# Filling TensorE's early waits with products of the identity, in a fused MLA, Hyena and MoE layer

## Chip, cores and metric

The kernel runs on one core of one Trainium2 chip. The metric is the device time of one execution in microseconds (us); lower is better. One execution was profiled; its times are counted from the first instruction of its span.

## What is computed

One layer of a diffusion backbone over 512 latent tokens and 256 context tokens of width 1024, all in f32. The part that the change touches is the very beginning:

```python
mod  = (silu(c) @ w_mod + b_mod).reshape(B, 6, D)
modc = (silu(c_ctx) @ w_mod + b_mod).reshape(6, D)
h  = modulate(rmsnorm(x, norm_mix), mod[:, 0], mod[:, 1])
hc = modulate(rmsnorm(ctx, norm_mix), modc[0], modc[1])
proj = h @ w_in + b_in
...
attention, Hyena convolution, merge, router, 64 experts, final norm
```

The change adds products whose result nobody reads; what is computed stays the same.

## The kernel before

The program is one long unrolled kernel. Tiles are allotted from pools, and the framework derives every wait from the tiles that an instruction reads and writes. A tile that lies in PSUM takes one bank. The order of instructions on each engine is laid out when the program is built, by a planner that simulates times. While `pinned[0]` is true, though, TensorE's products and transposes that go through the helpers `mm` (line 92) and `flip` (line 95) keep the order in which the code names them, and so do the loads that go through `fetch` (line 191). ScalarE's and VectorE's instructions are not held in this way.

The stage in question is the first 60 us. The code names it in one list (lines 374 to 425). For each q from 0 to 7:

- `mod_load(q)` fetches two tiles `wm` of 512 KB with 256 columns of `w_mod`. Six such tiles exist, so three q's can be under way.
- `mod_rows(q)` (line 207) multiplies silu of both conditioning vectors by those columns. The product `pm` is split into four groups of 32 output partitions (`mod_parts`, eight calls of `mm`; an f32 product is two passes on TensorE, each with a weight load, so 16 passes are recorded). ScalarE copies `pm` into a slice of `tit` (line 213). Two further products `ptm` with `cols32` (line 216, four passes) sum the four groups and turn the row into columns. VectorE adds the bias into `sh` (line 217).
- the pool `pm` has one bank, so the next q's products wait until the copy has read it.

The order of the q's on TensorE is 0, 4, 1, 5, 2, 6, 3, 7: shift and scale of the same 256 columns come one after the other. After each pair, `scales(k)` makes the factors `A`, and `streams(k, "l")` and `streams(k, "c")` transpose two column blocks of the normed tokens against the identity (`pxl`, eight passes; `pxc`, four), apply shift and scale on ScalarE (line 336), and split them into a high and a low part (lines 105 and 106). `both_mm(j)` (tiles `p`) multiplies the split tokens by two blocks of `w_in`, in twelve products of 512 or 256 columns in the type fp32r. Products `ps` belong to a small sine layer. `normed("l")` works on ScalarE and VectorE and precedes `mod_rows(0)`; TensorE has nothing to do before that. `ident` is a 128x128 f32 identity that GpSimd builds at the start.

Products with the identity as the moving operand occur elsewhere too: `srkv` and `srq` (line 477) multiply a 128x128 f32 tile by `ident`. In `mix` (line 815) one PSUM tile is cut in two halves of 256 columns: `po` is copied out by ScalarE at line 828, and then products with `ident` write the other half.

Of the kernel before, what the change touches and what calls it, by code (L numbers as in the profile page):

```python
# [51 lines left out]
def kernel(ctx: ExitStack, tc: tile.TileContext, x, ctxt, wmod, bmod, win, wuq, wuk, wuv, wba, wbh,  # L52
# [24 lines left out]
    def bank(name, n=512, tag="b1"):  # L77
        p, bufs = pspool[tag]
        return p.tile([128, 512], F32, name=name, tag=tag, bufs=bufs)[:, :n]
# [7 lines left out]
    def pin(i):  # L87
        if pinned[0]:
            tc.keep_in_program_order(i)

    def mm(o, lhsT, rhs, start=True, stop=True):
        pin(pe.matmul(o, lhsT, rhs, start=start, stop=stop))  # L92
# [26 lines left out]
    ident = const.tile([128, 128], F32, name="ident")  # L119
# [6 lines left out]
    def v(col, n=1, p=128):  # L126
        return vec[:p, col:col + n]

    def rsqrt(pool, ms, name):

        shp = list(ms.shape)
        a = pool.tile(shp, F32, name=name + "_a", tag="rq_a", bufs=2)
        s = pool.tile(shp, F32, name=name + "_s", tag="rq_s", bufs=2)
        r = pool.tile(shp, F32, name=name + "_r", tag="rq_r", bufs=4)
        dve.tensor_scalar(a, ms, EPS, None, ALU.add)
        act.activation(s, a, AF.Sqrt)
        dve.reciprocal(r, s)
        dve.tensor_tensor(s, r, r, ALU.mult)
        dve.tensor_tensor(s, s, a, ALU.mult)
        dve.tensor_scalar(s, s, -0.5, 1.5, ALU.mult, ALU.add)  # L140
        dve.tensor_tensor(r, r, s, ALU.mult)
        return r
# [39 lines left out]
    def mod_parts(pm, w):  # L182


        for j in range(8):
            g = 32 * (j % 4)
            mm(pm[g:g + 32], sc32[:, j], w(j), j < 4, j >= 4)

    def fetch(dst, src):

        tc.keep_in_program_order(sp.dma_start(dst, src))

    def mod_load(q):
        wmt[q] = [mp.tile([128, 4, 256], F32, name=f"wm{q}{h}", tag="wm", bufs=6) for h in range(2)]
        for h in range(2):
            fetch(wmt[q][h], wmod[q, :, 4 * h:4 * h + 4])
# [8 lines left out]

    pinned[0] = True

    def mod_rows(q):
        pm = bank(f"pm{q}", 256, "pm")
        mod_parts(pm, lambda j: wmt[q][j // 4][:, j % 4, :])  # L210

        row = tit[:, q % 4].rearrange("p r c -> p (r c)")
        act.copy(row, pm)
        pt = bank(f"ptm{q}", 4, "ms")
        for i in range(2):
            mm(pt[:, 2 * i:2 * i + 2], row[:, i * 128:(i + 1) * 128], cols32[:, 0:2])
        dve.tensor_tensor(sh[:, 2 * q:2 * q + 2, :], pt.rearrange("p (i c) -> p i c", c=2),
                          v(V_BM + 2 * q, 2).unsqueeze(2).to_broadcast([128, 2, 2]), ALU.add)
# [95 lines left out]
    def normed(nm):  # L314
        na = 2 * len(xs[nm])
        ms = mp.tile([128, na], F32, name=f"ms{nm}")
        for a in range(na):

            sq = (hT if nm == "l" else hTc)[1][:, 0:D // (128 * na)].rearrange("p j n -> p (j n)")
            act.activation(sq, xs[nm][a // 2][:, a % 2], AF.Square, scale=1.0 / 32.0, accum_out=ms[:, a:a + 1])  # L320
        rs = rsqrt(mp, ms, f"rs{nm}")
        for a in range(na):
            xi = xs[nm][a // 2][:, a % 2]
            dve.tensor_scalar(xi, xi, rs[:, a:a + 1], None, ALU.mult)
# [57 lines left out]
    for d, src in ((embt, emb), (w1t, fw1), (w2t, fw2)):  # L382
        fetch(d, src)
    normed("l")
    mod_rows(0)
    mod_load(5)
    mod_rows(4)
    mod_load(2)
    for k in range(2):
        fetch(w3t[64 * k:64 * k + 64], fw3)  # L390
    scales(0)
    streams(0, "l")
    normed("c")
    mod_rows(1)
    mod_load(6)
    streams(0, "c")
# [1005 lines left out]
    spare = []  # L1402
# [250 lines left out]
```

## Time and profile before

| What | us |
|---|---|
| median of 3 runs | 1358.63 |
| lowest, highest of the 3 | 1353.99, 1840.8 |
| the profiled execution, own time | 1358.62 |
| its span, first to last instruction | 1356.8 |
| TensorE busy | 1279.0 |
| VectorE busy | 1064.2 |
| ScalarE busy | 864.9 |

The span and what lies around it (1.8 us) make the profiled execution's time. PE stands for TensorE's products, PEld for its weight loads, DVE for VectorE, ACT for ScalarE, POOL for GpSimd, SP for SyncE, which issues the loads here. A busy PE is not a PE at its peak, since products are pipelined. "PEclk" is the share of TensorE's full clock that the profile reports as granted.

### The profile page before, as it was taken

How to read it: one execution, taken by the hardware profiler on the slowest of the kernel's cores; microseconds unless marked ns; L12 is line 12 of the kernel's file. 1: busy time of each engine (PE TensorE's matmuls, PEld its weight loads, DVE VectorE, ACT ScalarE, POOL GpSimd, SP SyncE). 2: the span in 40 equal slices, each digit the busy share in tenths (PEclk: the TensorE clock that was granted, in tenths of full speed). 3: DMA queues.
4: the chain of work that ended last, by engine and by line, in shares of the span. 5: the costliest groups of instructions: out<-in, count | busy, mean ns of one | idle time of the engine just before them, and what ended most of it. 6: DMA issues, size and time to landing. Idle time of an engine off the chain costs nothing.

```text
span 1356.8 us, 19380 instructions
## 1 busy us (share of the span) xinstructions
PE 1279.0 (94%) x6910; PEld 1049.9 (77%) x6910; DVE 1064.2 (78%) x1700; ACT 864.9 (64%) x1281; POOL 225.3 (17%) x215
## 2 busy tenths in 40 slices
PE   5999999998999999999999999999999999999970
PEld 3687777887777788778888888888888887888750
DVE  3667768995656558768989989988998998889845
ACT  5555553334655235448878787887887778878751
POOL 0000100001242323221112111121111111111120
PEclk9998999998999999899999999999999999999995
DMA  9533566633301464648999998899998999999944
GB/s 330 196 117 125 189 237 230 232 125 114 119 24 56 163 205 167 275 184 290 327 315 321 331 326 296 308 307 329 328 322 299 330 306 331 306 310 329 308 108 173
DMA packets 80903, 328.60 MB, mean 242 GB/s; under 512 B 13507, under 2 KB 15059, under 8 KB 53412
## 3 DMA queue, kind: packets, MB, share of 16 engines
q1 hardware_dynamic: 67300, 301.00, 61.8%
q0 software_dynamic: 11200, 22.14, 8.4%
q10 hardware_dynamic: 2304, 4.20, 0.8%
q8 instruction: 55, 0.90, 0.3%
q14 instruction: 44, 0.36, 0.1%
HBM read 292.71 MB, written 52.97 MB: 255 GB/s over the span
## 4 chain that ended last, share of the span: by engine, by line
PE 53%; DMA 6%; DVE 3%; ACT 2%; issue 2%; POOL 0%; POOLq 0%; DVEq 0%; SPq 0%; ACTq 0%
PE pge L92 24%; PE pye L92 12%; PE pxe L1265 5%; PE pxe L1266 4%; DMA accd<-Ye,ixe 4%; PE pgsh L92 2%; PE pba L92 2%; DMA accd<-Ys,ixs 1%; PE pbh L92 1%; PE pte L95 1%; PE pout L92 1%; PE pysh L92 1%; DMA rsg<-in_wsgu_dram 1%; PE sle L92 1%; DVE fa L1512 0%
## 5 line engine op out<-in xcount | busy, mean ns | idle before, releaser
L1099 POOL DMA_INDIRECT accd<-Ye,ixe x64 | 114.8, 1794 | 596.1 <-ACT Ye L1098 273.0
L1265 PE MATMUL pxe<-oge,h2h 128*128 128x256 f32 x512 | 131.0, 288 | 0.1
L1266 PE MATMUL pxe<-oge,h2l 128*128 128x256 f32 x512 | 127.9, 282 | 0.0
L1265 PEld LDWEIGHTS pxe<-oge,h2h 128*128 128x128 f32 x512 | 97.2, 190 | 3.9 <-issue 0.5
L1266 PEld LDWEIGHTS pxe<-oge,h2l 128*128 128x128 f32 x512 | 97.0, 189 | 3.3
L1098 ACT COPY Ye<-pye 128x1024 f32<-128x1024 f32 x64 | 65.0, 1015 | 8.6 <-PE pye L92 6.4
L790 DVE TENSOR_REDUCE st<-S 128x1 f32<-128x768 f32 x32 | 30.5, 955 | 21.9 <-PE S L92 21.2
L1071 ACT ACTIVATE aae<-pge 128x256 f32<-128x256 f32 x64 | 24.7, 385 | 26.1 <-PE pge L92 25.9
L794 ACT ACTIVATE P<-S,st 128x768 f32<-128x768 f32 x32 | 28.8, 902 | 12.6 <-DVE st L790 10.5
L1246 DVE TENSOR_TENSOR oge<-iot,posm 128x256 fp32r<-128x256 f32 x64 | 23.5, 420 | 10.1 <-PE pxe L1266 9.7
L1072 DVE SCALAR_TENSOR_TENSOR aae<-aae,wge,pge 128x256 f32<-128x256 f32 x64 | 30.5, 476 | 1.1 <-ACT aae L1071 0.4
L811 PE MATMUL pT<-ident,P 128*128 128x128 f32 x192 | 29.7, 276 | 0.0
L92 PE MATMUL po<-PT,V 128*64 128x256 f32 x192 | 29.1, 389 | 0.0
L812 DVE COPY PT<-pT 128x384 f32<-128x384 f32 x32 | 17.6, 549 | 12.5 <-PE pT L811 12.4
L811 PEld LDWEIGHTS pT<-ident,P 128*128 128x128 f32 x192 | 22.1, 140 | 6.2 <-issue 3.1
L812 ACT COPY PT<-pT 128x384 f32<-128x384 f32 x32 | 15.2, 476 | 17.1 <-PE pT L811 16.8
L95 PE MATMUL pte<-ident,aae 128*128 128x128 f32 x128 | 24.4, 272 | 0.0
L92 PE MATMUL pm<-wm,sc 128*32 128x256 f32 x128 | 14.0, 571 | 11.0 <-DMA wm<-in_wmod_dram 11.0
L92 PE MATMUL pgsh<-shguh,sx 128*128 128x512 f32 x64 | 23.8, 441 | 0.0
L572 DVE SCALAR_TENSOR_TENSOR u<-raw,vec,u 128x512 f32<-128x512 f32 x24 | 17.9, 748 | 6.7 <-ACT u L570 6.2
L95 PEld LDWEIGHTS pte<-ident,aae 128*128 128x128 f32 x128 | 17.3, 140 | 7.0
L1512 DVE TENSOR_TENSOR fa<-fa,modE 128x1024 f32<-128x1024 f32 x4 | 4.9, 1220 | 21.0 <-DMA fa<-accd 21.0
(6788 smaller groups left out, 4650.9 us busy)
## 6 DMA issues: line engine op xcount, KB each, us to landing
gu0e<-in_wgu_dram SPq DMA_DIRECT2D x64, 1024.0 KB
gu1e<-in_wgu_dram SPq DMA_DIRECT2D x64, 1024.0 KB
de<-in_wd_dram SPq DMA_DIRECT2D x64, 1024.0 KB
wn<-in_wmod_dram SPq DMA_DIRECT2D x16, 1024.0 KB
wm<-in_wmod_dram SPq DMA_DIRECT2D x16, 512.0 KB
rg<-in_win_dram SPq DMA_DIRECT2D x32, 256.0 KB
rhy<-in_win_dram SPq DMA_DIRECT2D x24, 256.0 KB
specd<-fX POOLq DMA_DIRECT2D x4, 1024.0 KB, 4.8
```

Source lines behind the costliest of these rows:

```text
L92: pin(pe.matmul(o, lhsT, rhs, start=start, stop=stop))
L95: pin(pe.transpose(o, i, idn))
L790: dve.tensor_reduce(st[:, 0:1], S[:, 0:NKEY], AX.X, ALU.max, negate=True)
L794: act.activation(P, S[:, 0:NKEY], AF.Exp, bias=st[:, 0:1], accum_out=rsum[a][:, h % 2:h % 2 + 1])
L811: pe.transpose(pT[:, i * 128:(i + 1) * 128], P[:, kt * 128:(kt + 1) * 128], ident)
L812: (dve.tensor_copy if k3 else act.copy)(PT[:, 3 * k3:3 * k3 + 3, aa * 128:(aa + 1) * 128], pT.rearrange("p (k q) -> p k q", k=3))
L1071: pin(act.activation(self.aa, pg[:, 0:FF], AF.Silu))
L1072: dve.scalar_tensor_tensor(self.aa, self.aa, self.wg, pg[:, FF:], ALU.mult, ALU.mult)
L1098: act.copy(Y, py)
L1099: gp.indirect_dma_start(out=accd, out_offset=bass.IndirectOffsetOnAxis(ap=self.ix, axis=0), in_=Y, in_offset=None, compute_op=ALU.add, bou ...
L1265: pe.matmul(o, h2h[:, a, js], oh, start=(a % 2 == 0), stop=False)
L1266: pe.matmul(o, h2l[a][:, js], oh, start=False, stop=(a % 2 == 1))
```

## The change

28 products of the identity with itself are put on TensorE in front of `mod_rows(0)`, into a bank of the pool `pm`. In every `mod_rows`, three more are put between ScalarE's copy of `pm` and the two products `ptm`. They write columns 256 to 383 of the same PSUM tile whose columns 0 to 255 hold `pm`; the tile now takes the whole 512 columns of its bank by name.

```diff
+    def idle(o, n):
+
+        for _ in range(n):
+            mm(o, ident, ident)
+
     def mod_rows(q):
-        pm = bank(f"pm{q}", 256, "pm")
+        pm = bank(f"pm{q}", 512, "pm")
+        spare, pm = pm[:, 256:384], pm[:, 0:256]
         mod_parts(pm, lambda j: wmt[q][j // 4][:, j % 4, :])
 
         row = tit[:, q % 4].rearrange("p r c -> p (r c)")
         act.copy(row, pm)
+        idle(spare, 3)
         pt = bank(f"ptm{q}", 4, "ms")
...
     normed("l")
+    idle(bank("pidle", 128, "pm"), 28)
     mod_rows(0)
```

## Rows read from the trace of the kernel before

**Rows 1.** The page: the span, and granted clock in 40 slices of it
```profile
span 1356.8 us, 19380 instructions
...
PEclk9998999998999999899999999999999999999995
```

**Rows 2.** Stretches of 10 us: length, busy time of each engine, PEclk, DMA share, GB/s
```profile
10.00:20.00 10.00, 7.92 (x52) 4.50 (x56) 4.48 (x15) 6.27 (x13) 0.00 (x0) 1.00 1.02 410
20.00:30.00 10.00, 7.91 (x49) 4.54 (x49) 5.95 (x17) 5.78 (x13) 0.00 (x0) 1.00 1.04 310
30.00:40.00 10.00, 8.85 (x49) 3.90 (x47) 4.44 (x9) 5.41 (x11) 0.00 (x0) 1.00 1.01 366
...
50.00:60.00 10.00, 9.01 (x50) 6.48 (x50) 6.38 (x15) 4.05 (x10) 0.00 (x0) 0.83 0.15 54
...
70.00:80.00 10.00, 10.00 (x52) 8.49 (x51) 5.42 (x15) 7.11 (x13) 0.31 (x1) 1.00 0.47 167
...
590.00:600.00 10.00, 8.27 (x36) 6.57 (x36) 8.27 (x8) 6.36 (x9) 6.40 (x3) 0.83 0.50 168
```

**Rows 3.** PE's timeline: start, us, instruction, count, [idle before it <- releaser]
```profile
10.96 2.25 PE L92 MATMUL pm<-wm,sc 128*32 128x256 f32 x16 [10.96 <-DMA wm<-in_wmod_dram]
13.70 1.01 PE L92 MATMUL ptm<-cols,tit 128*128 128x2 f32 x4 [0.49 <-ACT tit L213]
...
17.99 1.95 PE L95 MATMUL pxl<-ident,xl 128*128 128x128 f32 x8
19.87 1.94 PE L92 MATMUL pm<-wm,sc 128*32 128x256 f32 x16
...
24.25 0.45 PE L95 MATMUL pxc<-ident,xc 128*128 128x128 f32 x1 [0.94 <-PE ptm L92]
...
40.57 0.77 PE L92 MATMUL p<-hTh,wkv140h 128*128 128x512 f32 x1
...
44.50 0.39 PE L92 MATMUL p<-hTh,wkv140h 128*128 128x512 f32 x1
...
46.59 1.03 PE L95 MATMUL pxl<-ident,xl 128*128 128x128 f32 x8
47.56 1.07 PE L92 MATMUL pm<-wm,sc 128*32 128x256 f32 x16
49.12 0.61 PE L92 MATMUL ptm<-cols,tit 128*128 128x2 f32 x4 [0.49 <-ACT tit L213]
...
53.04 1.07 PE L92 MATMUL ps<-s1o,w2t 64*64 64x512 f32 x2 [0.26 <-DVE sh L217]
```

**Rows 4.** GpSimd's timeline: the instruction that completes the identity
```profile
1.36 0.28 POOL masks.py:199 TENSOR_SCALAR_AFFINE_SELECT ident<-ident 128x128 f32<-128x128 f32 x1
```

**Rows 5.** PE's timeline: f32 products with the identity, and what follows them
```profile
83.49 1.05 PE L92 MATMUL srkv<-ident,rrkv 128*128 128x128 f32 x8
84.30 0.36 PE L92 MATMUL fpb<-sd002h,tfth 128*128 128x256 f32 x1
...
118.01 1.91 PE L92 MATMUL srq<-ident,rrq 128*128 128x128 f32 x8
119.57 0.56 PE L92 MATMUL fpa<-sd010l,tfth 128*128 128x256 f32 x1
```

**Rows 6.** Timeline: a copy of one half of a bank, products into the other
```profile
454.23 0.37 ACT L828 COPY ot<-po 128x256 f32<-128x256 f32 x1 [3.12 <-PE po L92]
...
454.74 0.68 PE L92 MATMUL po<-ident,rr 128*128 128x128 f32 x4 [0.61 <-ACT ot L828]
```

**Rows 7.** Timelines of ACT and of DVE around `mod_rows(4)` and `mod_rows(1)`
```profile
16.70 0.37 ACT L213 COPY tit<-pm 128x256 f32<-128x256 f32 x1 [3.05 <-PE pm L92]
...
21.87 0.37 ACT L213 COPY tit<-pm 128x256 f32<-128x256 f32 x1 [0.49 <-PE pm L92]
...
23.41 1.41 DVE L324 TENSOR_SCALAR xc<-xc,rsc_r 128x1024 f32<-128x1024 f32 x2
```

**Rows 8.** PE's timelines after idle time: around 590 us, and the longest near 320 us
```profile
592.84 0.53 PE L92 MATMUL pge<-ge00h,XTe00h 128*128 128x512 f32 x1 [1.67 <-ACT XTe00h L105]
...
322.58 1.22 PE L92 MATMUL pv<-wuvh,kvnh 128*128 128x512 f32 x2 [4.07 <-ACT wuvh L105]
```

## Prediction

> **What bounds the kernel now.** I read the page first: span and granted clock [rows 1]. TensorE is granted full clock in nearly every slice, so a warm-up can only matter in a short stretch. Then stretches of 10 us [rows 2]. From 10 to 40 us the DMA engines are busy all the time (share 1.01 to 1.04) and PE for 7.9 to 8.9 us of each 10; from 70 us on PE is busy throughout. Whatever the first 60 us lose or win is therefore handed on, if PE is what holds them up. To see that, I read PE's timeline [rows 3]. The first products `pm` start at 10.96 us, when the first `wm` has landed. After that no wait in front of PE's products in these rows is put down to a DMA; they are short waits for ScalarE's copy (0.49 us) or for VectorE. So from 11 us on, the end of this stage is set by PE's chain, with ScalarE's copies in it, and the loads run just ahead of it.
>
> One thing in these rows contradicts the clock column. PEclk says 1.00 from 10 to 40 us [rows 2], yet the same instructions take twice as long as later: eight transposes `pxl` 1.95 us at 17.99 and 1.03 at 46.59, sixteen passes `pm` 1.94 at 19.87 and 1.07 at 47.56, four passes `ptm` 1.01 at 13.70 and 0.61 at 49.12 [rows 3]. A product of 512 columns listed with 0.77 us at 40.57 is listed with 0.39 at 44.50. I read this as the lower level (1.2 GHz) until some time between 40.57 and 44.50, before the first clock record, and the upper (2.4 GHz) after. In 50 to 60 us PEclk is 0.83, so it fell once more there. The change is aimed at this.
>
> **The change, part by part.**
>
> *The 28 products in front.* Each f32 product with `ident` is two passes: `srkv` with eight passes is followed 0.81 us later (83.49 to 84.30), at full clock, so 0.101 us per pass; `srq` with eight passes is followed after 1.56 us (118.01 to 119.57), at half clock, so 0.195 [rows 5]. 56 passes cost 5.7 us at full and 10.9 at half clock. They can start when GpSimd has finished the identity, 1.36 + 0.28 = 1.64 us [rows 4]; I take 1.7. PE has nothing else until 10.96. All at half clock they end at 12.6 and delay the first `pm` by 1.6 us; with a rise after as much dense work as preceded the one in rows 3 (44.50 - 40.57 = 3.9 us, 20 passes), the other 36 take 3.6 us and they end at 9.2, hidden behind the load. I take the second: cost nothing, and the clock is up when `pm` begins.
>
> *The three products in every `mod_rows`.* They are six passes: 0.61 us at full and 1.17 at half clock. The question is whether they run beside the copy or behind it. They write the bank that the copy reads. The nearest case is `mix`: the copy of one half of a bank starts at 454.23, takes 0.37 and ends at 454.60; the products into the other half start at 454.74, and their 0.61 us of waiting is put down to that copy [rows 6]. So they wait for the copy, as `ptm` does (0.49 us, rows 3), and `ptm`, next in PE's fixed order, starts only after them. The gap stays idle and the six passes stand on PE's chain. The Trainium skill, "PSUM — Partial Sum Buffer", section "PSUM bank collisions raise a hardware error", asks for the same: accesses of two engines to one bank and quadrant are to be kept apart by bank, not by address. By it every `mod_rows` pays the whole price; with no such rule only what exceeds the 0.49 us gap would be paid. Bounds for one set: 0.12 us (full clock, beside the copy) to 1.17 us (half clock, behind it). I take 0.61 or 1.17 by the clock.
>
> *Does the clock stay up?* With full clock, `pm` takes about 1.0 us and the next `wm` comes no sooner, since the DMA engines are full. PE would run out of work where it is now busy: the pair 0 and 4 would be done with its transposes near 17.9 us, 2 us ahead of the 19.87 at which the next `pm` starts now [rows 3]. In the trace, the clock fell in 50 to 60 us [rows 2] after a run of `pm`, `ptm`, transposes and the `ps` of 53.04, with gaps of only 0.26 to 0.49 us [rows 3]; and it was down for a part of 590 to 600 us [rows 2], where PE had been idle for 1.67 us before 592.84 [rows 8]. Both are denser than what the loads leave to PE between 17 and 25 us, even with six extra passes. I therefore take the clock to fall there, and to rise again in `both_mm`, as now.
>
> *The sum.* (a) `mod_rows` 0, 4 and 1: the faster products gain 0.9 us each and `ptm` 0.4, the extra passes take 0.61; but ScalarE has its own work (the copy for 1 comes at 21.87 after other casts) and the context transposes wait for VectorE, whose scaling of `xc` only starts at 23.41 [rows 7]; PE now idles 0.94 us for it at 24.25 [rows 3]. Gains and losses before that point end in this wait: 0. (b) `mod_rows` 5, 2 and 6 at half clock: 3 x 1.17 = 3.5 us on the chain. (c) `mod_rows` 3 and 7 at full clock: 2 x 0.61 = 1.2, of which the waits of 0.26 us near them absorb two: 0.7. Sum 0 + 3.5 + 0.7 = 4.2 us. After 60 us nothing is added; PE is full from 70 us, so the delay is handed on whole. 1358.62 + 4.2 = 1362.8. The profiled execution's time is the median of the runs shown (1358.62 and 1358.63), so this is also the forecast for the median.
>
> The SP queue: its loads of later `wm` wait for `pm` to free a tile. `pm` itself moves little in (a), and in (b) the loads are already ahead; I take nothing for it.
>
> **The rivals.**
>
> *The clock holds* through the stage (the other side, faster). Then from 24 us on the chain loses its doubling: `pm` of 5, 2 and 6 gain 0.9 each, their `ptm` 0.4 each, eight transposes 0.9, two sets of four 0.5 each, the sine product 0.9, the first half of `both_mm` 1.7, and 1.7 more if the fall in 50 to 60 us goes as well: 10.1. The extra passes take 5 x 0.61 = 3.0 of it, and ScalarE's and VectorE's order around the copies holds back some 1.5: -5.6 us, so 1353. It decides at about 25 us: full clock there means this case. For it: the chain would stay filled better than now. Against it: the two falls above. The Trainium skill states the rule behind this case in "TensorE: Matmul & The Clock Gate", section "Why this matters for your kernels": keep matmuls coming without long gaps and the clock stays up. By that rule the time would be this rival's, as gaps here are short; the fall in 50 to 60 us, with gaps under half a microsecond, speaks against it.
>
> *The identity products do not raise the clock.* No rise in rows 3 follows f32 products; the eight `pxl` and the `pm` behind them from 17.99 to 21.8 are dense and raise nothing. Then the front costs 1.6, (a) becomes 3 x 1.17 less the 0.94 of idle, 2.6; with (b) and (c): 1.6 + 2.6 + 4.2 = 8.4 us, 1367.
>
> *Beside the copy.* If nothing orders the extra passes behind it, each set costs 0.49 less: 3 x 0.68 + 2 x 0.12 = 2.3 us, 1360.9. Against it stands rows 6.
>
> *The planner.* ScalarE's and VectorE's order is laid out anew at build. One wait like the 4.07 us near 320 [rows 8] gained or lost somewhere makes 1354.5 or 1362.7 around no change.
>
> **How the numbers follow.** Forecast 0.45; clock holds 0.2; no rise 0.15; beside the copy 0.1; planner 0.1. The range runs from 1352, a microsecond below the clock that holds, to 1369, two above the one that never rises; what is left out is the planner adding to either end. 2% is 27 us, about what a measurement of this kernel can tell from no change; only a planner's order that goes wrong or right in the long stretches could move that much. Faster by over 2%: 0.03; within: 0.94; slower: 0.03.
>
> **What would show it.** Right: the first `pm` still at about 11 us and listed near 1.1 us; extra passes starting right after each copy, `ptm` 0.6 or 1.2 us later than copy plus 0.1; `pm` of 5, 2 and 6 near 1.9 us; the first `both_mm` at about 44 instead of 40.57. Wrong: `pm` at 1.0 us from 25 to 40 (the clock holds), the first `pm` after 12 us (no rise), extra passes starting before the copy ends.

## The result, and the profile after

The changed kernel takes 1365.59 us (median of 6 runs, 1362.19 to 1368.96). The kernel before took 1357.37 beside it. The ratio is 1.0069, with a 95% interval of 1.0053 to 1.0085: about 9 us slower, inside 2%. The ratio leaves out one slow run of the kernel before (1840.8 us); by the two medians the difference is 8.2 us. The forecast was 1362.8, with 1352 to 1369 as its range. A second timing of the changed kernel (below) gave 1366.99 and 1.0066 [1.0049, 1.0083]. So direction and range held, and the forecast loss of 4.2 us was half of what came. That the time lies within the range is luck in part: most of the loss arose in a place where the prediction had added nothing, and the stage that it reckoned with cost less than forecast.

The page after, the same two lines as in [rows 1]. The profiled execution took 1368.96 us, the longest of the six; its span is 10.4 us longer than that of before:

```profile
span 1367.2 us, 19572 instructions
...
PEclk8998999998999999999999999999999999999995
```

PE's timeline after, the rows that answer to [rows 3] (start, us, instruction, count, idle time before it and releaser):

```profile
1.70 8.09 PE L92 MATMUL pidle<-ident 128*128 128x128 f32 x56 [1.70 <-POOL ident masks.py:199]
11.63 0.64 PE L92 MATMUL pm<-wm,sc 128*32 128x256 f32 x8 [1.84 <-DMA wm<-in_wmod_dram]
12.80 0.64 PE L92 MATMUL pm<-wm,sc 128*32 128x256 f32 x8 [0.54 <-DMA wm<-in_wmod_dram]
13.94 0.94 PE L92 MATMUL pm<-ident 128*128 128x128 f32 x6 [0.49 <-ACT tit L219]
14.71 0.51 PE L92 MATMUL ptm<-cols,tit 128*128 128x2 f32 x4
...
21.09 0.64 PE L92 MATMUL pm<-wm,sc 128*32 128x256 f32 x8 [1.22 <-DMA wm<-in_wmod_dram]
22.23 1.65 PE L92 MATMUL pm<-ident 128*128 128x128 f32 x6 [0.49 <-ACT tit L219]
23.67 0.85 PE L92 MATMUL ptm<-cols,tit 128*128 128x2 f32 x4
...
32.51 1.07 PE L92 MATMUL pm<-wm,sc 128*32 128x256 f32 x16
...
39.39 1.08 PE L92 MATMUL pm<-wm,sc 128*32 128x256 f32 x8 [0.64 <-DMA wm<-in_wmod_dram]
...
43.12 0.77 PE L92 MATMUL p<-hTh,wkv140h 128*128 128x512 f32 x1
```

The 56 passes in front take 8.09 us, between the 5.7 (all at full clock) and 10.9 (all at half) of the prediction: the clock rose while they ran. The first `pm` are at full rate, 0.64 us for eight passes. Each set of three products starts when the copy `tit` is done (0.49 us of waiting in the rows shown), so it stands behind the copy. A set holds PE for 0.77 us at full clock (13.94 to 14.71) and 1.44 at half (22.23 to 23.67). The clock falls between 21.09 and 22.23, is up again at 32.51 (16 passes in 1.07) and down again at 39.39 (eight in 1.08). Six waits of PE, 5.8 us in all, are now put down to the loads (of them 1.84, 0.54, 1.22 and 0.64 us in these rows); in the kernel before only the first `pm` had one.

The stretches after, to be held against [rows 2] (length, busy us of PE, PEld, DVE, ACT, POOL; PEclk, DMA share, GB/s):

```profile
10.00:20.00 10.00, 6.40 (x68) 4.11 (x68) 4.32 (x14) 5.85 (x12) 0.00 (x0) 1.00 1.02 409
20.00:30.00 10.00, 7.56 (x44) 5.06 (x45) 5.72 (x15) 6.11 (x14) 0.00 (x0) 0.60 1.01 281
30.00:40.00 10.00, 7.59 (x62) 4.78 (x60) 4.59 (x11) 4.13 (x7) 0.00 (x0) 0.84 1.01 316
40.00:50.00 10.00, 9.51 (x58) 8.03 (x54) 4.12 (x9) 4.20 (x7) 0.00 (x0) 0.70 0.71 276
```

PEclk now shows what the durations show: up, down to 0.60, partly up, down. Over these 40 us the stage wins something by faster products and pays the sets and the waits for loads.

**Where the 10 us come from.** I followed one instruction at a time through both traces. PE's timeline before, at three places:

```profile
62.69 0.48 PE L92 MATMUL p<-hTh,wkv141h 128*128 128x512 f32 x1
...
213.33 0.39 PE L92 MATMUL pg<-hTh,wg20h 128*128 128x512 f32 x1
...
316.20 0.42 PE L92 MATMUL pkn<-kvnh,wukh 128*128 128x384 f32 x1
```

and after:

```profile
65.06 0.48 PE L92 MATMUL p<-hTh,wkv141h 128*128 128x512 f32 x1
...
214.89 0.39 PE L92 MATMUL pg<-hTh,wg20h 128*128 128x512 f32 x1
...
326.29 0.42 PE L92 MATMUL pkn<-kvnh,wukh 128*128 128x384 f32 x1
```

The first of these is the start of `both_mm(4)`, which this text and the expectations call the fourth block of `both_mm`, counting from 0: it comes 2.4 us later than before. The first `pg` of weight block 20, a gate product, comes 1.6 us later. At the first `pkn`, a product of the attention, the delay is 10.1 us, and at the end of PE's work 11.7. So most is lost between 213 and 316 us, in the Hyena convolution and the gate products, which the diff does not touch. The waits of PE there say how. Before, waits of PE from 190 to 350 us (who waited for whom, total us, times, longest):

```profile
PE pv L92 <- ACT wuvh L105: 4.1, 1, 4.1
PE pkn L92 <- DVE sk L647: 0.8, 1, 0.8
PE pq L92 <- DVE KT11l L106: 0.7, 1, 0.7
```

After, the same view and stretch:

```profile
PE py L92 <- DVE Z L639: 4.7, 1, 4.7
PE pv L92 <- ACT wuvh L105: 4.1, 1, 4.1
PE pkn L92 <- DVE sk L655: 0.8, 1, 0.8
```

One wait is new: `py`, the products of the inverse transform, waits 4.7 us for VectorE's `Z`. PE's timeline around it, before:

```profile
312.71 3.73 PE L92 MATMUL py<-tit,Z 128*128 128x128 f32 x32
317.72 0.44 PE L92 MATMUL pkn<-kvnh,wukh 128*128 128x384 f32 x1 [0.76 <-DVE sk L647]
```

and after:

```profile
314.73 0.39 PE L92 MATMUL pg<-hTh,wg131l 128*128 128x512 f32 x1
319.84 6.70 PE L92 MATMUL py<-tit,Z 128*128 128x128 f32 x32 [4.72 <-DVE Z L639]
...
327.82 0.44 PE L92 MATMUL pkn<-kvnh,wukh 128*128 128x384 f32 x1 [0.76 <-DVE sk L655]
```

At 314.73 the last of the gate products `pg` that filled PE runs, and the last 32 `py` are not ready. PE stands for 4.72 us; in that gap the clock falls (at 319.0 us by the trace's clock records), and the same 32 passes take 6.70 us in place of 3.73. The stretch after, with PEclk at 0.71:

```profile
320.00:330.00 10.00, 7.85 (x38) 7.22 (x38) 5.27 (x10) 2.47 (x4) 1.08 (x2) 0.71 0.03 11
```

Together 4.72 + 2.97 = 7.7 of the 8.5 us that are lost between 213 and 316.

Why `Z` is late can be read one step up, in the products `za` of the last forward transform and the copy and sums that follow. PE's timeline before, at its last `za` of block 110:

```profile
289.43 0.28 PE L92 MATMUL za<-zT110h,tftl 128*128 128x256 f32 x1
```

VectorE's timeline before, from its first `EO` of this block to the `Z` behind it:

```profile
288.98 0.68 DVE L605 TENSOR_TENSOR EO<-za,zcp 128x512 f32<-128x512 f32 x1
...
311.22 0.68 DVE L631 TENSOR_TENSOR Z<-AB 128x512 f32<-128x512 f32 x1
```

After, PE's timeline at the same `za`:

```profile
300.82 0.27 PE L92 MATMUL za<-zT110h,tftl 128*128 128x256 f32 x1
```

and VectorE's after:

```profile
300.00 0.69 DVE L613 TENSOR_TENSOR EO<-za,zcp 128x512 f32<-128x512 f32 x1 [0.78 <-ACT zcp L611]
...
319.09 0.70 DVE L639 TENSOR_TENSOR Z<-AB 128x512 f32<-128x512 f32 x1
```

In the order laid out for the changed kernel the last `za` come 11.4 us later on PE, behind gate products that run ahead of them. VectorE's chain from `EO` to `Z`, with the other work that it does in between, takes 22.2 us before and 19.1 after, so `Z` starts 7.9 us later, and PE has used up the gate products that covered this chain before. The sequence of tiles on PE between 70 and 700 us differs between the two traces in 68 places; between two executions of the changed kernel it differs in 2. The sequences of VectorE and ScalarE differ as well, in some 45 and 22 places. The order is fixed at build, by a planner that simulates times; that the products of the identity change the order by shifting these simulated times is an inference.

### The profile page after: what moved, and what is told of

Same layout as the page of the kernel before. It is cut to its first block, busy times and chain, and to the rows that moved or that the text cites. A ratio compares the mean times of both kernels' runs of the same rounds, so it can differ in the third digit from the quotient of the medians.

```text
span 1367.2 us, 19572 instructions
## 1 busy us (share of the span) xinstructions
PE 1288.2 (94%) x7014; PEld 1062.6 (78%) x7014; DVE 1064.1 (78%) x1700; ACT 865.2 (63%) x1281; POOL 223.4 (16%) x215
## 4 chain that ended last, share of the span: by engine, by line
PE 51%; DMA 6%; DVE 4%; ACT 2%; issue 2%; POOL 0%; DVEq 0%; POOLq 0%; SPq 0%; ACTq 0%
PE pge L92 24%; PE pye L92 12%; PE pxe L1273 4%; PE pxe L1274 4%; DMA accd<-Ye,ixe 4%; DMA accd<-Ys,ixs 1%; PE pgsh L92 1%; PE pout L92 1%; PE pte L95 1%; PE pysh L92 1%; PE pba L92 1%; DMA gt<-gated 1%; PE sle L92 1%; PE pbh L92 1%; DMA rsg<-in_wsgu_dram 0%
## 5 line engine op out<-in xcount | busy, mean ns | idle before, releaser
L1254 DVE TENSOR_TENSOR oge<-iot,posm 128x256 fp32r<-128x256 f32 x64 | 23.6, 421 | 10.1 <-PE pxe L1274 9.9
L92 PE MATMUL py<-tit,Z 128*128 128x128 f32 x128 | 17.9, 307 | 4.7 <-DVE Z L639 4.7
L92 PEld LDWEIGHTS py<-tit,Z 128*128 128x128 f32 x128 | 17.7, 223 | 5.4 <-DVE Z L639 5.1
```

## The experiments

The theory after this reading: the order laid out anew costs about 8 us, the added products little. The rival: the products cost it, in the stage and by what they push along. In the table, "order" is PE's order after 70 us as the trace shows it, and "wait" the wait of `py` for `Z`. Ratios are to the kernel before on the same chip, with 95% intervals.

| kernel | in front | behind or beside the copies | order | wait, us | ratio |
|---|---|---|---|---|---|
| changed | 28 | 24 behind | new | 4.7 | 1.0069 [1.0053, 1.0085] |
| front28 | 28 | 0 | new | 4.7 | 1.0089 [1.0074, 1.0104] |
| four3 | 28 | 25 behind | new | 4.7 | 1.0077 [1.0064, 1.0090] |
| one7 | 0 | 1 behind | another | 4.5 | 1.0072 [1.0056, 1.0087] |
| beside | 28 | 24 beside | another | 6.9 | 1.0057 [1.0042, 1.0071] |
| beside1 | 28 | 8 beside | near before's | none | 1.0001 [0.9992, 1.0010] |
| front16 | 16 | 0 | before's | none | 0.9995 [0.9984, 1.0006] |
| gaps01256 | 28 | 15 behind | before's | none | 1.0036 [1.0024, 1.0048] |
| less1 | 28 | 23 behind | before's | none | 1.0016 [1.0005, 1.0028] |
| plus2 | 28 | 26 behind | before's | none | 1.0004 [0.9990, 1.0017] |

**The products in front alone.**

```diff
-        idle(spare, 3)
```

> Only the 28 products in front; none in mod_rows. Behind 60 us the planner's order is nearly that of the changed kernel. Planner theory (the order laid out anew between 110 and 340 us costs some 7 us, whatever runs on the chip before): the fourth both_mm starts no later than in the kernel before (62.7 us, or 1 to 4 us sooner), yet the whole is 2 to 7 us slower. Product theory (the loss is the passes behind the copies): no loss, 0 to 4 us faster.

Measured: 1370.63 us. With nothing left in the gaps the kernel is as slow as the changed one, or slower: some 12 us by the ratio, more than the 2 to 7 of the theory, while the product theory expected no loss. In its trace the fourth block of `both_mm` is 1.7 us late, where it was expected no later than before, and the first `pkn` 8.2, with the same wait:

```profile
PE py L92 <- DVE Z L638: 4.7, 1, 4.7
```

**Sixteen in front, none in the gaps.**

```diff
-        idle(spare, 3)
+        if q in (9,):
+            idle(spare, 3)
...
-    idle(bank("pidle", 128, "pm"), 28)
+    idle(bank("pidle", 128, "pm"), 16)
```

> Only 16 products in front. The order of every engine is that of the kernel before. Both theories: within 2 us of the kernel before. What is open is whether the clock rises and what it is worth: 32 passes end near 7 us, the first pm starts near 11, so the clock should be down again by the first or second pm; gain 0 to 2 us at the fourth both_mm.

Measured: 1357.38 us, no difference. No q is 9, so nothing is left in the gaps. PE's order is that of before. The clock rises in front (the trace's clock records have it at 7.8 us) and falls at 11.2, so nothing is won either (the fourth block of `both_mm` is 0.6 us late, where a gain of 0 to 2 was expected): products in front raise the clock, and it does not last.

**Products in five of the eight gaps.**

```diff
-        idle(spare, 3)
+        if q in (0, 1, 2, 5, 6):
+            idle(spare, 3)
```

> The changed kernel with the three products only in mod_rows 0, 1, 2, 5 and 6 (not 3, 4, 7), and the 28 in front; behind 60 us the order of every engine is that of the kernel before. Planner theory: total 0 to 3 us slower than the kernel before, and the same delay from the fourth both_mm to the end. Product theory: five eighths of the loss of some 8 us, so 4 to 6 us slower.

Measured: 1363.32 us, 4.9 us slower by the ratio. That is what the product theory expected (4 to 6), not the planner theory (0 to 3). PE's order is that of before, and the delay is made in the stage alone: 7.2 us at the fourth block of `both_mm`, 7.25 at the first `pkn`. PE's stretches in this kernel:

```profile
10.00:20.00 10.00, 7.46 (x56) 4.97 (x55) 3.92 (x12) 3.90 (x8) 0.00 (x0) 0.70 1.02 406
20.00:30.00 10.00, 7.20 (x42) 4.88 (x44) 5.12 (x16) 6.49 (x13) 0.00 (x0) 0.50 0.94 277
30.00:40.00 10.00, 8.62 (x60) 5.73 (x53) 2.57 (x7) 4.62 (x10) 0.00 (x0) 0.60 1.02 322
40.00:50.00 10.00, 8.18 (x42) 5.36 (x42) 6.99 (x16) 5.59 (x9) 0.00 (x0) 0.57 0.85 305
```

The clock is at half for most of 14 to 51 us, as it was before the change; four of the five sets run at half clock and one at full, 4 x 1.44 + 0.77 = 6.5 us, and the stage is 7.2 late. So with the clock down the delay is close to the full price of the sets; in places PE also waits longer for ScalarE's copy, 2.80 us at most.

**The same kernel once more.** The edit is the one above.

> The same kernel as gaps01256 once more, one look. If the cost of the stage hangs on when the clock falls and rises (theory): the fourth both_mm block comes at another delay than the +7.2 us of the first look, between +2 and +7, with the low stretches of the clock elsewhere, and the delay of the rest follows it one to one, since the order is that of the kernel before. If the cost is in the products by themselves (rival): +7 again, within 0.5.

Measured in one execution: the fourth block is again 7.3 us late, the first `pkn` 6.4, although the clock's low stretches lie otherwise (12.9 to 23.1 and 26.5 to 53.8). My theory of a delay that changes with the clock's phase expected +2 to +7; the rival's +7 is what came. This does not rule the theory out, since the clock was down for nearly as much of the stage both times (PEclk from 11 to 62 us is 0.66 in the first trace and 0.63 in this one). The interval of the timing above (3.3 to 6.5 us) says that not all executions lose this much.

**Products beside the copy**, into the bank of `ptm` in place of that of `pm`.

```diff
-        pm = bank(f"pm{q}", 512, "pm")
-        spare, pm = pm[:, 256:384], pm[:, 0:256]
+        pm = bank(f"pm{q}", 256, "pm")
...
-        idle(spare, 3)
-        pt = bank(f"ptm{q}", 4, "ms")
+        pt = bank(f"ptm{q}", 512, "ms")
+        spare, pt = pt[:, 256:384], pt[:, 0:4]
+        idle(spare, 3)
```

> The three products of each mod_rows write the bank of ptm instead of the bank that ScalarE's copy reads; the 28 in front stay. If the bank is what holds them back, they start right behind pm, before the copy ends, the gap of 0.49 us is filled, and ptm starts some 0.4 us later than the copy's end instead of 0.77 to 1.44; the fourth both_mm starts 0 to 2 us sooner than in the changed kernel. If not, they wait as before. The order behind 60 us is another one again, so the total can lie anywhere from 5 us faster to 9 us slower.

Measured: 1365.62 us. PE's timeline at the first set:

```profile
12.15 0.64 PE L92 MATMUL pm<-wm,sc 128*32 128x256 f32 x8 [0.53 <-DMA wm<-in_wmod_dram]
12.72 0.94 PE L92 MATMUL ptm<-ident 128*128 128x128 f32 x6
13.49 0.51 PE L92 MATMUL ptm<-cols,tit 128*128 128x2 f32 x4
```

ScalarE's timeline there:

```profile
12.87 0.37 ACT L218 COPY tit<-pm 128x256 f32<-128x256 f32 x1
```

In a bank of their own the passes start at 12.72, before the copy has begun at 12.87, and `ptm` follows without a wait. So it was sharing the tile, and with it its bank, that put them behind the copy; tile and bank were not tried apart. The stage ends 1.8 us ahead of before (fourth block of `both_mm`), which is what the change was after, and 4.2 us ahead of the changed kernel's, where 0 to 2 was expected. But this kernel has yet another order: `py` waits 6.9 us for `Z`, the first `pkn` is 9.3 us late, and the time is no better than the changed kernel's.

**A single product of the identity in the whole kernel**, behind the copy of `mod_rows(7)`.

```diff
-        idle(spare, 3)
+        if q in (7,):
+            idle(spare, 1)
...
-    idle(bank("pidle", 128, "pm"), 28)
```

> No products in front, and a single product of the identity (2 passes, some 0.25 us of TensorE at 47 us) behind the copy of mod_rows(7) alone; the layout of the unpinned order comes out different from the kernel before in 80 places of TensorE's list from about 110 us on. If the order laid out anew is what costs (theory): 4 to 9 us slower than before (ratio 1.003 to 1.0065), with the first pkn 4 to 9 us later than 316.2 while the fourth both_mm block stays within 0.6 us of 62.69. If the passes themselves cost (rival): at most 0.6 us slower, ratio within 1.0005.

Measured: 1367.85 us, 9.8 us slower than before, for two passes, some 0.25 us by the price of a set. PE's timeline:

```profile
313.95 5.25 PE L92 MATMUL py<-tit,Z 128*128 128x128 f32 x32 [4.50 <-DVE Z L639]
325.75 1.22 PE L92 MATMUL pv<-wuvh,kvnh 128*128 128x512 f32 x2 [5.48 <-ACT wuvh L105]
```

The wait of 4.50 for `Z` is there, and the wait of `pv` that [rows 8] show with 4.07 is 5.48. The place was not quite as expected: the first `pkn` is only 2.8 us late, since the stage itself came out 1.5 us early and the delay goes on growing to 8.7 us by the first `pge`, the first product of the experts (592.84 before [rows 8], 601.53 here). The price in the whole was above the 4 to 9 us of the theory; the rival's 0.6 is far off. This order differs from the changed kernel's too (64 places), so what it shows is that a new order can cost all of it, not that this very order did.

**One product beside each copy**, as in the run beside with `idle(spare, 1)`.

> The 28 products in front, and one product of the identity per mod_rows instead of three, written into the bank of ptm so that it runs beside ScalarE's copy. Late order differs from the kernel before in 23 places of TensorE's list (80 to 90 where the order is laid out wholly anew). If products beside the copy are free and only the new order cost in the run with three (theory): stage at least not slower than before, fourth both_mm block 0 to 2 us ahead of 62.69, and a time of 1355 to 1358.5. If the early products cost wherever they stand (rival): 2 us or more slower, 1360 or above.

Measured: 1358.02 us, no difference. In its trace the stage ends 1.9 us early and the first `pkn` 0.7 early, but the median shows none of it. This was the candidate to beat both kernels; it equals the kernel before.

**The changed kernel once more.**

> The changed kernel once more, one look. If the order costs a fixed amount (theory): the first pkn falls behind by 6.5 to 8.5 us more than the fourth both_mm block does, whatever delay the early stage has this time (+2.4 at first). If the loss at 250 to 316 us came from the early delay (rival): it scales with that delay.

Measured in one execution: 1371.14 us. The fourth block of `both_mm` is 3.55 us late, the first `pkn` 9.85: 6.3 more, against 7.7 more in the execution above and just under the 6.5 to 8.5 that was expected. The early delay grew by 1.2 us and the later loss did not grow with it. In both traces the delays at the first `pg` of block 20 agree within 0.1 us (1.56 and 1.62), and from there to `pkn` both lose 8.2 to 8.5.

**One product more than the changed kernel**, chosen for an order that was expected to be that of before.

```diff
-        idle(spare, 3)
+        idle(spare, (3, 3, 3, 4, 3, 3, 3, 3)[q])
```

> The changed kernel with one product of the identity more: four in place of three in mod_rows(3). With it the layout of TensorE's unpinned order comes out exactly as that of the kernel before. If the order laid out anew carries most of the loss (theory): this kernel is faster than the changed one by 5 to 8 us although it does more, 1359 to 1362.5 (ratio 1.001 to 1.0035); its fourth both_mm block is 2 to 4 us late, the first pkn is late by the same within 1 us, and TensorE does not wait 4.7 us for Z in front of py. If the products carry it (rival): at least as slow as the changed kernel, 1365 or above, ratio 1.0055 to 1.009.

Measured: 1369.56 us. The premise was wrong: the trace shows the changed kernel's order, not that of before, and its wait:

```profile
PE py L92 <- DVE Z L639: 4.7, 1, 4.7
```

So this run tells nothing between the theories; it is one more kernel with the new order and its loss. Beside it the changed kernel was timed.

> The changed kernel itself, timed beside four3 on the same chip. Both theories: 1364 to 1370, ratio 1.005 to 1.009, with the wait of 4.7 us for Z in front of py in its trace.

Measured: 1366.99 us, with the wait of 4.7 us. In this trace the stage is only 0.24 us late at the fourth block of `both_mm`, yet the first `pkn` is 6.4 late.

**The changed kernel with the order of before**, by two products more.

```diff
-        idle(spare, 3)
+        idle(spare, (3, 3, 3, 4, 3, 3, 3, 4)[q])
```

> The changed kernel with two products of the identity more: four in place of three in mod_rows(3) and in mod_rows(7), 26 behind the copies in all. At build, TensorE's unpinned order comes out as that of the kernel before; if so, TensorE does not wait 4.7 us for Z in front of py. If the order laid out anew carries most of the loss (theory): faster than the changed kernel by 4 to 8 us although it does more, 1359 to 1362.5 (ratio 1.001 to 1.0035), the fourth both_mm block 0.5 to 4.5 us late and the first pkn late by the same within 1 us. If the products carry it (rival): as slow as the changed kernel or slower, 1365 or above, ratio 1.0055 to 1.009.

Measured: 1358.21 us; PE's order differs from before's in 2 places of the trace, as two executions of one kernel do (VectorE's in 2, ScalarE's in none). The waits of PE from 190 to 350 us are those of before, in this view and to the tenth:

```profile
PE pv L92 <- ACT wuvh L105: 4.1, 1, 4.1
PE pkn L92 <- DVE sk L655: 0.8, 1, 0.8
PE pq L92 <- DVE KT11l L106: 0.7, 1, 0.7
```

and the last `py` runs without a wait and at full rate:

```profile
311.16 3.73 PE L92 MATMUL py<-tit,Z 128*128 128x128 f32 x32
```

It does all that the changed kernel does and two products more, and is 7.4 to 8.8 us faster than the two medians of the changed kernel, a little below the range of the theory. The stage was not late this time: the fourth block of `both_mm` comes 0.3 us early and the first `pkn` 1.55 early, 1.3 us apart where 1 was expected.

**The same with one product less than the changed kernel.**

```diff
-        idle(spare, 3)
+        idle(spare, (4, 2, 3, 2, 4, 2, 3, 3)[q])
```

> The changed kernel with 23 products behind the copies in place of 24 (four in mod_rows 0 and 4, two in 1, 3 and 5, three in 2, 6 and 7); at build, TensorE's unpinned order comes out as that of the kernel before. Theory as for the run with 26: 1359 to 1362.5, first pkn as late as the fourth both_mm block within 1 us. Rival: a product less can give back 0.25 us at most, so 1365 or above.

Measured: 1359.87 us. The fourth block of `both_mm` is 1.8 us late and the first `pkn` 1.7: the delay is handed on unchanged where the order is that of before.

The two last kernels stand on either side of the changed one in what they add, and differ from it in the order. Their mean ratio is 1.0010, the changed kernel's 1.0068 over its two timings: 0.0058 of 1357.7 us, 7.9 us, go to the order. What is left to the products is 0.0010, or 1.4 us (intervals -1.4 to +2.3 and +0.7 to +3.8). The size depends on the pair: gaps01256, the third kernel with products in the gaps and the order of before, leaves 0.0032 or 4.3 us to the order; front28 against front16, neither with anything in the gaps, gives it 0.0094 or 12.8 us. All of these have the same sign, and every kernel that loses 7 us or more waits 4.5 us or longer for `Z`.

## Why the prediction was right and wrong

**The front: right.** The clock rises during the products in front, in every kernel that has them (between 4.6 and 8 us by the clock records), and they end at 9.79 us in the profiled execution, ahead of the first load. This margin does not always hold: in other traces they end as late as 11.17 us, and in that of changed_timed the first `pm`, at 11.20, follows them without waiting for a load. The rise itself rules out the rival by which identity products do not raise the clock.

**The bank: right.** The sets wait 0.49 us for the copy and stand on PE's chain, as [rows 6] had it, and the run with a tile and bank of their own shows that sharing is the cause. The rule cited from the Trainium skill, "PSUM — Partial Sum Buffer", section "PSUM bank collisions raise a hardware error", to keep two engines apart by bank and not by address, is in line with both. What happens when two engines do meet in one bank no run here shows.

**The price of a set: too low.** The 0.61 and 1.17 us taken from [rows 5] were 0.77 and 1.44. A pass with `ident` on both sides took 0.128 us at full clock and 0.24 at half here, against 0.101 and 0.195 for `srkv` and `srq`. A nearer row stood in [rows 3]: eight transposes `pxl` are followed after 0.97 us at full clock (46.59 to 47.56) and 1.88 at half (17.99 to 19.87), 0.121 and 0.235 per pass.

**The clock: right in kind, not in time.** It fell after 21 us as forecast, so the rival in which it holds is out. It rose again sooner than in `both_mm`, and fell once more: `pm` of 5 ran at half clock as forecast (1.94 us at 26.03), `pm` of 2 at full (1.07 at 32.51), that of 6 half and half. The rule of the Trainium skill, "TensorE: Matmul & The Clock Gate", section "Why this matters for your kernels", by which short gaps keep the clock up, is contradicted by this trace: it fell with no gap longer than 1.22 us on PE since the first `pm`. The traces of the changed kernel differ in when the clock falls and rises; by what, I have not shown.

**The sum of the stage: too high.** The three traces of the changed kernel have the fourth block of `both_mm` 2.37, 3.55 and 0.24 us late, where 4.2 was forecast. In the first of them term (a), put at 0, came to 0.33 us (`pm` of 5 at 26.03, before at 25.70); (b), put at 3.5, to 2.2 (the first `both_mm` at 43.12, before at 40.57); (c), put at 0.7, to -0.2. Sets cost more than reckoned, and faster products gave part of it back: `pm` of 2 takes 1.07 us in place of about 1.94. By plus2 and less1, with the order of before, only 0.5 to 2.2 us reach the end; by gaps01256 it is 4.9.

**The failed step: "After 60 us nothing is added".** Some 8 us are added there: a wait of 4.72 us of `py` for `Z`, and 2.97 us because the clock falls in that wait and the 32 passes behind it run at about half rate. This is the rival of the planner, which I gave a chance of 0.1 and a price of one wait like the 4.07 us of [rows 8]. The mechanism was right, the price half, since the fall of the clock behind such a wait was not in it; and it came on top of the stage's cost, not in place of it. The prediction also had the means to weigh it higher: the order of ScalarE, VectorE and of all unpinned products is laid out from simulated times, and 28 + 24 products could be expected to shift these times.

Open: the first `pm` starts 0.03 to 1.05 us later in all kernels with products in front than in the kernel before. SP starts to issue the `wm` loads at 2.12 us with and without them. Whether this is the scatter of the loads or something that the products cause was not tried. Why 15 products in the gaps cost more than 23 or 26 can be read in part from the granted clock. PEclk from 11 to 62 us is 0.66 and 0.63 in the two traces of gaps01256, with the fourth block of `both_mm` 7.2 and 7.3 us late. It is 0.80 in less1 (1.8 late) and 0.83 in plus2 (0.3 early); in the three traces of the changed kernel it is 0.77, 0.83 and 0.87 (3.55, 2.37 and 0.24 late). So in these traces the stage is on the whole less late where more of it ran at full clock. What makes the clock fall at one time or another stays open.

## What to carry to other kernels

Where a planner lays out the order from simulated times, an edit, even one product of 0.25 us, can change the order a long way off. Give that a chance and a price of its own before the sums of the edited stage, and follow a few instructions through both traces before crediting the edit with the difference. To measure an edit by itself, find a neighbouring variant of it that keeps the old order, as the one with 26 products here.

Products that are to warm TensorE beside a copy need a PSUM tile, and with it a bank, which the copy does not read. Even then they won nothing that could be measured here (1.0001 with the order nearly that of before).

## What was not expected of the hardware

- A wait of 4.7 us of PE cost 7.7 us: the clock fell within it and the next 32 passes took 6.70 us, not 3.73. In the kernel one7 the wait of 4.50 was followed by 5.25.
- The clock rose while PE ran f32 products of the identity back to back (by the clock records at 4.6 to 7.9 us, in every trace with 32 or 56 such passes in front). No row of before had shown a rise behind such products.
- f32 passes of 128x128 with the identity do not all take the same time: 0.101 us at full clock for `srkv`, 0.121 for the transposes `pxl`, 0.128 for the identity with itself. What makes the difference was not tried.
